# The mLSTM's queries and keys by seven-product groups, with the convolution in place

## The chip, the core and the metric

The kernel runs on one core of a Trainium2 chip. The metric is device time in microseconds (us) from launch to end. Five engines work side by side, each with its own queue of instructions that it takes strictly in the order written: TensorE (PE, matmul; its weight loads are shown as PEld), VectorE (DVE), ScalarE (ACT), GpSimd (POOL) and SyncE (SP), which issues the weight loads from main memory.

## The reference

A decoder trunk of two layers over 512 positions of width 1024, in float32. Cut to what matters here:

```python
for l in range(DEPTH):                                    # 2
    proj = x @ w_in[l]                                    # (512, 1024) @ (1024, 8200)
    (r_q, r_k, r_v, r_g, m_qk, m_v, m_o, m_i, m_f, g_a, g_b) = split(proj)
    # retention: 4 heads, rotary on r_q and r_k, head norm, silu(r_g), projection -> y_ret
    qk_c = silu(causal_depthwise_conv(m_qk, conv_w[l], conv_b[l]))   # width 4, along positions
    mq, mk = qk_c[..., :512], qk_c[..., 512:]             # 4 heads of 128
    # mLSTM: 4 heads of 128 x 256, head norm, sigmoid(m_o), projection -> y_ml
    mix = (sigmoid(g_a + b) * y_ret + sigmoid(g_b + b) * y_ml) @ w_out[l]
    x = layer_norm(alpha * x + mix)
    hidden = silu(gate) * up                              # x @ w_gate_up, 2 x 2816 columns
    x = layer_norm(alpha * x + hidden @ w_down[l])
```

## The kernel before

**Precision.** A number is split into two parts, hi (a cast on ScalarE, L201 for weights) and lo (number minus hi, a subtraction on the vector engine in `lo_of`, L133). A product is three matmuls: hi·hi, hi·lo, lo·hi. The weights come as 512 KB units (tile wraw) and are split into whi and wlo, four units ahead of their use (`LOOK = 4`).

**Three forms of product.** `feat` (L260 to L262) takes one unit and makes 128 output features for all 512 positions, laid out with features on partitions: 24 matmuls of 512 columns. `tok_units` (L351 to L353) makes 512 features with positions on partitions, four units for four PSUM banks. `quad` (L318) takes four units at once as a 2 x 2 block matrix and forms the product of 512 input halves and position halves with seven block products instead of eight (the scheme of Strassen and Winograd): 7 x 24 matmuls of 256 columns. Its operands are two weight blocks as they are, B11 and B22, further B21, and the sums T1, T3, T2 (vector engine, L187, L189, L191) and T4 (GpSimd, L223). Its other side needs four sums of the input (tiles xs, made by `input_sums`), and its results are put together from the banks as they come (for the merge gate in `gate_ev`, tiles ga and gc). Before, `quad` serves the merge gates and the feed-forward projection.

**The stages of a layer.** For two pairs of heads each: retention's q and k (4 `feat`, rotated by `rot_evac`: tiles rqk, rt), its values (`tok_units`, split into rvh and rvl), its gate (`tok_units`). Then the same for the mLSTM: q and k (4 `feat`, each with its convolution in `conv_evac`: one copy, four vector steps, one Silu), values (mvh, mvl), gate. Then the merge gates (4 `quad`), the two output projections, W_out, layer norm, feed-forward, layer norm. A stage of `tok_units` uses the four PSUM banks of the stage ahead of it, so its first matmul waits until that stage's first block is evacuated.

**Side work.** What belongs to a head (scores, weighted sums, head norm, the loads of head outputs in `fetch`, the input sums) is written as generators in the queue `side`. The stages call `slot()` after each piece of matmul work (six matmuls in `tok_units`, six to twelve in the others), and each call advances the first generator by one step. In one layer, `input_sums` stands in this queue behind the first head's scores of retention's second pair. It has four quarters, each with two additions on GpSimd (L577, tile xs), four small vector operations (L583, tile sf), a cast on ScalarE (tile xs0h or xs1h) and a split (xs0l, xs1l).

**What sets the order.** On TensorE and SyncE the instructions stand as the program writes them. On the other three a scheduler puts them in order when the program is built, except inside the `quad` stages, where these too stand as written.

The lines shown have the numbers of the kernel before; those of the kernel after differ by a few (L133 is the same; L577 is L586, L583 is L592, L610 is L618, L741 and L745 are L747 and L751, L853 is L886).

Of the kernel before, what the change touches and what calls it, by code (L numbers as in the profile page):

```python
# [15 lines left out]
P = 128  # L16
# [37 lines left out]
def layer_plan():  # L54
# [34 lines left out]
    for j in range(2, FT, 2):  # L89
        for c in (0, DFF):  # L90
# [7 lines left out]
NUNIT = len(layer_plan())  # L98
QUADS = [layer_plan().index(("F", w, c + j * P)) for w, c, js in (("in", O_GA, (0, 4)), ("in", O_GB, (0, 4)),
                                                                  ("gu", 0, range(2, FT, 2))) for j in js]  # L100
UNIT_IF = layer_plan().index(("F", "if", 0))
# [3 lines left out]
def decoder_trunk(ctx: ExitStack, tc: tile.TileContext, wall, xT_in, x_in, pvec, lnp, rtab, out):  # L105
# [18 lines left out]
    def scratch(shape, name):  # L124
        return reg.tile(shape, F32, tag="sc", name=name, bufs=4)
# [115 lines left out]

    side = deque()

    def slot():
        while side:
            try:
                next(side[0])
                return
            except StopIteration:
                side.popleft()  # L250
# [120 lines left out]
    def tok_blocks(pms, sh, sl, kts, first, evac, within):  # L371

        ws = [take() for _ in kts]
        for b in range(NB):
# [8 lines left out]
            evac(b, pms[b])  # L383

    K8 = [(2 * i, 2 * i + 1) for i in range(KT // 2)]

# [159 lines left out]
    def fetch(od, his, los):  # L546

        for i in range(4):
            t = scratch([P, 2, S], "of")
            nc.gpsimd.dma_start(t, od[:, 2 * i : 2 * i + 2])  # L550
            yield
            yield
            hi, lo = (x[i // 2][:, 2 * i % 4 : 2 * i % 4 + 2] for x in (his, los))
            nc.scalar.copy(hi, t)
            yield
            lo_of(lo, t, hi)
            yield
# [13 lines left out]
    def input_sums(xh, xl, sh, sl):  # L571

        t1, t2 = slice(0, S // 2), slice(S // 2, S)
        for m in range(4):
# [6 lines left out]
            for i, a, b, op in ((0, a21, a22, ALU.subtract), (1, f[:, 0], a11, ALU.subtract),  # L581
                                (2, a11, a21, ALU.subtract), (3, f[:, 1], a12, ALU.add)):
                nc.vector.tensor_tensor(out=f[:, i], in0=a, in1=b, op=op)  # L583
            yield
            nc.scalar.copy(sh[:, :, m], f)
# [3 lines left out]
    def rest(n):  # L589
        for _ in range(n):  # L590
            yield

    for l in range(L):
# [70 lines left out]

        for p in range(2):
            qk = reg.tile([P, 4, S], F32, tag="qk", name="rqk")
            rots = [rot_evac(qk[:, i]) for i in range(4)]
# [27 lines left out]
            side.append(scores(qk, 0, boxes[0], *ret_weights(2 * p)))  # L695
            if p == 1:
                side.append(input_sums(xh, xl, *xs))
            if p == 0:
# [35 lines left out]

        def conv_evac(dst, ct):
            def ev(pm):
                cw = lambda i: pv[:, C_CW + 4 * ct + i : C_CW + 4 * ct + i + 1]
                u = scratch([P, 2, S], "cv")
                r, t = u[:, 0], u[:, 1]
                nc.scalar.copy(r, pm)  # L740
                nc.vector.tensor_scalar(out=t, in0=r, scalar1=cw(3), scalar2=pv[:, C_CB + ct : C_CB + ct + 1],  # L741
                                        op0=ALU.mult, op1=ALU.add)
                for i in (2, 1, 0):
                    d = 3 - i
                    nc.vector.scalar_tensor_tensor(out=t[:, d:], in0=r[:, : S - d], scalar=cw(i), in1=t[:, d:],  # L745
                                                   op0=ALU.mult, op1=ALU.add)
                nc.scalar.activation(dst, t, AF.Silu)  # L747
            return ev

        for p in range(2):  # L750
            qk = reg.tile([P, 4, S], F32, tag="qk", name="mqk")  # L751
            for i in range(4):
                feat(xh, xl, conv_evac(qk[:, i], (i % 2) * 4 + 2 * p + i // 2))
            boxes = [[None], [None]]
# [106 lines left out]

        ordered = {mybir.EngineType.Activation, mybir.EngineType.DVE, mybir.EngineType.Pool}
        with tc.manual_schedule(engines=ordered):
            for m in (0, 4):
                quad(xh, xl, *xs, gate_ev(sga, 0, m))
# [332 lines left out]
```

## Time and profile before

| | us |
|---|---|
| three runs | 1804.14, 1806.07, 1806.31 (median 1806.07) |
| profiled execution | 1806.1 (span of its instructions 1804.4) |
| TensorE busy | 1772.4 (98% of the span) |
| VectorE busy | 1263.8 (70%) |
| ScalarE busy | 794.3 (44%) |
| GpSimd busy | 420.6 (23%) |

An engine's busy share is a mean over stages of different kinds. What counts is where TensorE stands still and which engine it waits for there. In the rows, "out<-in" names the tiles, "x" counts instructions, and square brackets give the idle time ahead of an instruction with the engine (and tile) that ended it. Matmuls overlap, so the distance of two starts, not the duration of one, is the time that a matmul takes.

### The profile page before, as it was taken

The numbers are of one execution on the slowest core, as the hardware profiler recorded it, in microseconds if no ns is written. First come the engines' busy times: TensorE is split into PE (matmuls) and PEld (weight loads), VectorE is DVE, ScalarE is ACT, GpSimd is POOL, SyncE is SP. The second block draws the span as 40 slices with busy tenths as digits, with TensorE's granted clock in tenths as the row PEclk, the third lists the DMA queues.
The fourth block names the chain that finished last, engine by engine and source line by source line (L and its number), as shares of the span: only waits on it lengthen the run. The fifth ranks groups of instructions, "written<-read, shape, count | busy, mean of one in ns | idle before, by whom it ended". The sixth has DMA issues, their size and how long they took to land.

```text
span 1804.4 us, 26440 instructions
## 1 busy us (share of the span) xinstructions
PE 1772.4 (98%) x10616; PEld 1580.5 (88%) x10616; DVE 1263.8 (70%) x1686; ACT 794.3 (44%) x1148; POOL 420.6 (23%) x309
## 2 busy tenths in 40 slices
PE   9998999999999999999999999999999999999997
PEld 7887888998889999988898788889988899999886
DVE  6676666775459999963476856667755599999534
ACT  4434655554225444452244345556532254444410
POOL 2041100231001455620120400012310015554200
PEclk9999999999999999999999999999999999999999
DMA  7332322247332333362243233213463333333521
GB/s 247 91 97 94 109 79 94 71 140 248 98 116 89 127 95 101 106 214 94 86 160 94 93 99 112 89 64 117 127 236 101 109 106 94 106 118 106 198 70 47
DMA packets 72826, 209.43 MB, mean 116 GB/s; under 512 B 6616, under 2 KB 8536, under 8 KB 71680
## 3 DMA queue, kind: packets, MB, share of 16 engines
q1 hardware_dynamic: 62864, 168.32, 29.0%
q0 software_dynamic: 9840, 39.43, 6.4%
q8 instruction: 83, 1.36, 0.3%
q14 instruction: 39, 0.32, 0.1%
HBM read 190.93 MB, written 16.79 MB: 115 GB/s over the span
## 4 chain that ended last, share of the span: by engine, by line
PE 92%; DVE 5%; issue 1%; ACT 1%; DMA 1%; POOL 0%; SPq 0%; DVEq 0%; ACTq 0%
PE pm L318 25%; PE pm L351 9%; PE pm L352 8%; PE pm L353 8%; PE pm L262 7%; PE pm L260 7%; PE pm L261 7%; PE pa L318 4%; PE pa L352 3%; PE pa L351 3%; PE pa L353 3%; DVE wlo L133 1%; DVE sf L583 1%; PE pa L484 1%; PE pa L485 1%; PE pa L486 1%
## 5 line engine op out<-in xcount | busy, mean ns | idle before, releaser
L133 DVE TENSOR_TENSOR wlo<-wraw,whi 128x1024 fp32r<-128x1024 f32 (+2 forms) x404 | 569.8, 1423 | 231.3 <-ACT whi L201 228.8
L201 ACT CAST whi<-wraw 128x1024 fp32r<-128x1024 f32 x391 | 408.8, 1049 | 507.2 <-PE pm L261 133.9
L440 POOL TENSOR_TENSOR rs<-ve,nhalf 128x4 f32<-128x4 f32 (+1 forms) x32 | 32.2, 1006 | 525.1 <-DVE ve L439 525.1
L351 PE MATMUL pm<-whi,x0h 128*128 128x512 f32 x256 | 102.9, 402 | 8.2 <-DVE rvl L133 8.1
L351 PE MATMUL pm<-whi,x20h 128*128 128x512 f32 x256 | 103.2, 403 | 7.0 <-DVE rvl L133 7.0
L353 PE MATMUL pm<-wlo,x20h 128*128 128x512 f32 x256 | 100.9, 394 | 0.0
L352 PE MATMUL pm<-whi,x20l 128*128 128x512 f32 x256 | 100.8, 394 | 0.0
L353 PE MATMUL pm<-wlo,x0h 128*128 128x512 f32 x256 | 100.7, 393 | 0.0
L352 PE MATMUL pm<-whi,x0l 128*128 128x512 f32 x256 | 100.5, 393 | 0.0
L223 POOL TENSOR_TENSOR wraw<-wraw 128x1024 f32<-128x1024 f32 x28 | 67.4, 2408 | 110.1 <-issue 54.4
L1049 POOL TENSOR_TENSOR qa<-qa 128x512 f32<-128x512 f32 x20 | 42.8, 2141 | 142.5 <-DVE qa L1048 90.6
L318 PE MATMUL pm<-s1h,wlo 128*128 128x256 f32 x240 | 67.9, 283 | 0.0
L318 PE MATMUL pm<-x10h,whi 128*128 128x256 f32 x240 | 67.9, 283 | 0.0
L318 PE MATMUL pm<-x10h,wlo 128*128 128x256 f32 x240 | 67.9, 283 | 0.0
L318 PE MATMUL pm<-s0h,whi 128*128 128x256 f32 x240 | 67.9, 283 | 0.0
L318 PE MATMUL pm<-x11h,whi 128*128 128x256 f32 x240 | 67.9, 283 | 0.0
L318 PE MATMUL pm<-x10l,whi 128*128 128x256 f32 x240 | 67.9, 283 | 0.0
L318 PE MATMUL pm<-s0l,whi 128*128 128x256 f32 x240 | 67.9, 283 | 0.0
L318 PE MATMUL pm<-x11l,whi 128*128 128x256 f32 x240 | 67.9, 283 | 0.0
L318 PE MATMUL pm<-s1h,whi 128*128 128x256 f32 x240 | 67.9, 283 | 0.0
L318 PE MATMUL pm<-s0h,wlo 128*128 128x256 f32 x240 | 67.9, 283 | 0.0
L318 PE MATMUL pm<-x11h,wlo 128*128 128x256 f32 x240 | 67.9, 283 | 0.0
(511 smaller groups left out, 5573.3 us busy)
## 6 DMA issues: line engine op xcount, KB each, us to landing
wraw<-wall SPq DMA_DIRECT2D x307, 512.0 KB, 3.7
od<-ot POOLq DMA_DIRECT2D x16, 512.0 KB, 3.0
of<-od POOLq DMA_DIRECT2D x16, 512.0 KB, 4.9
gb<-lnp POOLq DMA_DIRECT2D x4, 1024.0 KB, 6.5
x1d<-xr POOLq DMA_DIRECT2D x8, 512.0 KB, 2.9
xr<-x1d POOLq DMA_DIRECT2D x8, 512.0 KB, 4.7
negm<-md POOLq DMA_DIRECT2D x2, 1026.0 KB, 7.1
xr<-xtok POOLq DMA_DIRECT2D x4, 512.0 KB, 6.6
```

Of the source, the lines that this page charges most:

```text
L133: nc.vector.tensor_tensor(out=out_lo, in0=full, in1=hi.bitcast(F32), op=ALU.subtract)
L201: nc.scalar.copy(hi, sum_t[i])
L223: nc.gpsimd.tensor_tensor(out=raw_t[u + 2], in0=raw_t[u], in1=raw_t[u + 3], op=ALU.add)
L260: nc.tensor.matmul(pm[:, c0:c1], lhsT=hi[:, k], rhs=xh[:, k, c0:c1], start=(k == 0), stop=False)
L261: nc.tensor.matmul(pm[:, c0:c1], lhsT=hi[:, k], rhs=xl[:, k, c0:c1], start=False, stop=False)
L262: nc.tensor.matmul(pm[:, c0:c1], lhsT=lo[:, k], rhs=xh[:, k, c0:c1], start=False, stop=(k == KT - 1))
L318: nc.tensor.matmul(pm, lhsT=x[:, j, k], rhs=y[:, k], start=go and n == 0, stop=j == 1 and k == 3 and n == 2, skip_group_check=not first)
L351: nc.tensor.matmul(pm, lhsT=sh(k)[:, a], rhs=hi[:, j], start=first, stop=False)
L352: nc.tensor.matmul(pm, lhsT=sl(k)[:, a], rhs=hi[:, j], start=False, stop=False)
L353: nc.tensor.matmul(pm, lhsT=sh(k)[:, a], rhs=lo[:, j], start=False, stop=last)
L440: nc.gpsimd.tensor_tensor(out=rs[:, :n], in0=ve[:, :n], in1=nhalf[:, :n], op=ALU.pow)
L1049: nc.gpsimd.tensor_tensor(out=v, in0=v, in1=u, op=ALU.subtract)
```

## The change

Four things:

1. The mLSTM's q and k of a pair of heads are made by one `quad` instead of four `feat`. `conv_ev` puts the results together in the tile mqk; then `conv` runs over each of the four blocks, reads mqk and writes its Silu back to the same place. The copy ahead of each convolution is gone. A `rest(7)`, seven empty steps, stands in the side queue ahead of the scores.
2. `input_sums` goes to a queue of its own, `slow`, which every fifth call of `slot()` advances. It is put there at the start of retention's second pair, four projections earlier than before. One of its three yields per quarter is gone.
3. `fetch` has one more empty step between load and cast, and one more behind the cast.
4. `QUADS` lists the mLSTM's blocks, so their units are loaded as four blocks of the 2 x 2 matrix; number and size of the loads stay.

```diff
-QUADS = [... (("in", O_GA, (0, 4)), ("in", O_GB, (0, 4)), ("gu", 0, range(2, FT, 2))) for j in js]
+QUADS = [... (("in", O_MQK, (0, 2)), ("in", O_GA, (0, 4)), ("in", O_GB, (0, 4)), ("gu", 0, range(2, FT, 2))) for j in js]
...
-    side = deque()
+    side, slow = deque(), deque()
+    SLOW = 5
+    turn = {"n": 0}
 
     def slot():
+        turn["n"] += 1
+        if slow and turn["n"] % SLOW == 0:
+            if next(slow[0], "end") == "end":
+                slow.popleft()
         while side:
...
             nc.gpsimd.dma_start(t, od[:, 2 * i : 2 * i + 2])
             yield
             yield
+            yield
             hi, lo = (x[i // 2][:, 2 * i % 4 : 2 * i % 4 + 2] for x in (his, los))
             nc.scalar.copy(hi, t)
+            yield
             yield
             lo_of(lo, t, hi)
...
                 nc.vector.tensor_tensor(out=f[:, i], in0=a, in1=b, op=op)
-            yield
             nc.scalar.copy(sh[:, :, m], f)
             lo_of(sl[:, :, m], f, sh[:, :, m])
...
         for p in range(2):
+            if p == 1:
+                slow.append(input_sums(xh, xl, *xs))
             qk = reg.tile([P, 4, S], F32, tag="qk", name="rqk")
...
             side.append(scores(qk, 0, boxes[0], *ret_weights(2 * p)))
-            if p == 1:
-                side.append(input_sums(xh, xl, *xs))
...
-        def conv_evac(dst, ct):
-            def ev(pm):
-                u = scratch([P, 2, S], "cv")
-                r, t = u[:, 0], u[:, 1]
-                nc.scalar.copy(r, pm)
...
+        def conv(x, ct):
+            cw = lambda i: pv[:, C_CW + 4 * ct + i : C_CW + 4 * ct + i + 1]
+            t = scratch([P, S], "cv")
+            nc.vector.tensor_scalar(out=t, in0=x, scalar1=cw(3), scalar2=pv[:, C_CB + ct : C_CB + ct + 1],
+                                    op0=ALU.mult, op1=ALU.add)
+            for i in (2, 1, 0):
+                d = 3 - i
+                nc.vector.scalar_tensor_tensor(out=t[:, d:], in0=x[:, : S - d], scalar=cw(i), in1=t[:, d:],
+                                               op0=ALU.mult, op1=ALU.add)
+            nc.scalar.activation(x, t, AF.Silu)
+
+        def conv_ev(qk):
+            t = {}
+            part = lambda i, h: qk[:, 2 * i : 2 * i + 2, h * HC : (h + 1) * HC]
+            two = lambda bank: bank.rearrange("p (j t) -> p j t", j=2)
+
+            def ev(name, banks):
+                if name == "p1":
+                    t["u"] = scratch([P, 2, 2, HC], "mu")
+                    nc.scalar.copy(t["u"][:, 0], two(banks["a"]))
+                elif name == "p5":
+                    nc.scalar.copy(t["u"][:, 1], two(banks["c"]))
+                elif name == "p7":
+                    nc.vector.tensor_tensor(out=part(1, 1), in0=t["u"][:, 1], in1=two(banks["d"]), op=ALU.subtract)
+                elif name == "p6":
+                    u, v = t["u"][:, 0], t["u"][:, 1]
+                    nc.vector.tensor_tensor(out=u, in0=two(banks["b"]), in1=u, op=ALU.add)
+                    nc.gpsimd.tensor_tensor(out=v, in0=v, in1=u, op=ALU.subtract)
+                    nc.gpsimd.tensor_tensor(out=part(1, 1), in0=part(1, 1), in1=u, op=ALU.subtract)
+                elif name == "p2":
+                    nc.scalar.copy(part(0, 0), two(banks["a"]))
+                    nc.vector.tensor_tensor(out=part(1, 0), in0=two(banks["e"]), in1=t["u"][:, 1], op=ALU.add)
+                elif name == "p4":
+                    nc.vector.tensor_tensor(out=part(0, 1), in0=two(banks["d"]), in1=t["u"][:, 0], op=ALU.add)
             return ev
 
         for p in range(2):
             qk = reg.tile([P, 4, S], F32, tag="qk", name="mqk")
+            with tc.manual_schedule(engines=ordered):
+                quad(xh, xl, *xs, conv_ev(qk))
             for i in range(4):
-                feat(xh, xl, conv_evac(qk[:, i], (i % 2) * 4 + 2 * p + i // 2))
+                conv(qk[:, i], (i % 2) * 4 + 2 * p + i // 2)
+            side.append(rest(7))
```

What this makes of the order at three places. First GpSimd, layer 0, from the rotations of retention's second pair (L610 before, L618 after) to the end of the input sums (xs). Before:

```order
L610 TENSOR_TENSOR rqk<-rqk,rt 128x512 x2
L543 DMA od<-ot 128x1024
L610 TENSOR_TENSOR rqk<-rqk,rt 128x512
L543 DMA od<-ot 128x1024
L610 TENSOR_TENSOR rqk<-rqk,rt 128x512
L577 TENSOR_TENSOR xs<-x0h,x0l 128x512 x8
```

After:

```order
L586 TENSOR_TENSOR xs<-x0h,x0l 128x512 x2
L447 TENSOR_TENSOR rs<-ve,nhalf 128x4
L618 TENSOR_TENSOR rqk<-rqk,rt 128x512
L586 TENSOR_TENSOR xs<-x0h,x0l 128x512
L618 TENSOR_TENSOR rqk<-rqk,rt 128x512
L586 TENSOR_TENSOR xs<-x0h,x0l 128x512
L550 DMA od<-ot 128x1024
L618 TENSOR_TENSOR rqk<-rqk,rt 128x512
L550 DMA od<-ot 128x1024
L618 TENSOR_TENSOR rqk<-rqk,rt 128x512
L586 TENSOR_TENSOR xs<-x0h,x0l 128x512 x4
```

Four of the eight additions have moved between the rotations; the other four still follow the last rotation in one piece.

Second the vector engine, layer 0, first pair of the mLSTM, from the last convolution steps (cv) to the first split of the values (mvl). Before, the end of the fourth convolution is mixed with the scores (pf, pp, qf):

```order
L741 TENSOR_SCALAR cv<-cv,pv_98 128x512
L762 TENSOR_SCALAR pf<-negm,cols 128x128
L745 SCALAR_TENSOR_TENSOR cv<-cv,pv_98 128x511
L133 TENSOR_TENSOR wlo<-wraw,whi 128x1024
L745 SCALAR_TENSOR_TENSOR cv<-cv,pv_98 128x510
L769 SCALAR_TENSOR_TENSOR pf<-pa,pf 128x384
L745 SCALAR_TENSOR_TENSOR cv<-cv,pv_98 128x509
```

After, from the group's last evacuation:

```order
L777 TENSOR_TENSOR mqk<-pm,mu 128x2x256
L747 TENSOR_SCALAR cv<-mqk,pv_98 128x512 x2
L751 SCALAR_TENSOR_TENSOR cv<-mqk,pv_98,cv 128x511 x2
L751 SCALAR_TENSOR_TENSOR cv<-mqk,pv_98,cv 128x510 x2
L751 SCALAR_TENSOR_TENSOR cv<-mqk,pv_98,cv 128x509 x2
L747 TENSOR_SCALAR cv<-mqk,pv_98 128x512 x2
L751 SCALAR_TENSOR_TENSOR cv<-mqk,pv_98,cv 128x511 x2
L751 SCALAR_TENSOR_TENSOR cv<-mqk,pv_98,cv 128x510 x2
L751 SCALAR_TENSOR_TENSOR cv<-mqk,pv_98,cv 128x509 x2
L133 TENSOR_TENSOR wlo<-wraw,whi 128x1024 x2
L795 TENSOR_SCALAR pf<-negm,cols 128x256
```

All sixteen steps now stand in one piece behind the last evacuation, two chains side by side, and the scores behind them.

Third the vector engine, layer 0, end of the third group of the merge gates, where the third or fourth head output load (of) is split (orl). Before:

```order
L853 TENSOR_TENSOR ga<-pm,ga 128x512
L133 TENSOR_TENSOR orl<-of,orh 128x1024
L133 TENSOR_TENSOR wlo<-wraw,whi 128x1024 x4
L843 TENSOR_TENSOR gc<-ga,pm 128x512
L133 TENSOR_TENSOR wlo<-wraw,whi 128x1024
```

After:

```order
L886 TENSOR_TENSOR ga<-pm,ga 128x512
L133 TENSOR_TENSOR wlo<-wraw,whi 128x1024
L133 TENSOR_TENSOR orl<-of,orh 128x1024
L133 TENSOR_TENSOR wlo<-wraw,whi 128x1024 x3
L876 TENSOR_TENSOR gc<-ga,pm 128x512
L133 TENSOR_TENSOR orl<-of,orh 128x1024
```

One weight split has moved ahead of the load's split, and the last load's split (orl) has moved into the next group.

More of the change, by code (lines that the diff above doesn't have):

```diff
@@ L98 @@
 NUNIT = len(layer_plan())
-QUADS = [layer_plan().index(("F", w, c + j * P)) for w, c, js in (("in", O_GA, (0, 4)), ("in", O_GB, (0, 4)),
-                                                                  ("gu", 0, range(2, FT, 2))) for j in js]
+QUADS = [layer_plan().index(("F", w, c + j * P)) for w, c, js in (("in", O_MQK, (0, 2)), ("in", O_GA, (0, 4)),
+                                                                  ("in", O_GB, (0, 4)), ("gu", 0, range(2, FT, 2))) for j in js]
 UNIT_IF = layer_plan().index(("F", "if", 0))
@@ L383, in tok_blocks @@
             evac(b, pms[b])
+    ordered = {mybir.EngineType.Activation, mybir.EngineType.DVE, mybir.EngineType.Pool}
     K8 = [(2 * i, 2 * i + 1) for i in range(KT // 2)]
@@ L732, in decoder_trunk @@
         nc.gpsimd.dma_start(negm, md.unsqueeze(0).broadcast_to([P, NH, S + 1]))
-        def conv_evac(dst, ct):
-            def ev(pm):
-                cw = lambda i: pv[:, C_CW + 4 * ct + i : C_CW + 4 * ct + i + 1]
-                u = scratch([P, 2, S], "cv")
-                r, t = u[:, 0], u[:, 1]
-                nc.scalar.copy(r, pm)
[L741 to L747, printed above, removed]
+        def conv(x, ct):
[8 more added lines that the diff above has]
+            nc.scalar.activation(x, t, AF.Silu)
@@ L860, in gate_ev @@
             return ev
-        ordered = {mybir.EngineType.Activation, mybir.EngineType.DVE, mybir.EngineType.Pool}
         with tc.manual_schedule(engines=ordered):
+            assert not slow
             for m in (0, 4):
```

## Prediction

> **What bounds the kernel now.** I read the page first, then the waits of the tensor engine, then busy time by stage, last the rows around the places where the tensor engine stands still. The page:
>
> ```profile
> PE 1772.4 (98%) x10616; PEld 1580.5 (88%) x10616; DVE 1263.8 (70%) x1686; ACT 794.3 (44%) x1148; POOL 420.6 (23%) x309
> PE 92%; DVE 5%; issue 1%; ACT 1%; DMA 1%; POOL 0%; SPq 0%; DVEq 0%; ACTq 0%
> ```
>
> The tensor engine sets the end; the vector engine holds 5% of the chain that ended last. So a change pays by taking matmul time away, or a stop of the tensor engine. What it waits for (us in total, times, longest):
>
> ```profile
> PE pm L351 <- DVE rvl L133: 15.1, 4, 6.4
> PE pa L318 <- DVE wlo L133: 2.8, 2, 1.7
> ```
>
> The first row is mostly the start of retention's gate stage for the second pair of heads: its PSUM banks come free only when the vector engine has split the values (rvl). By stage (busy PE, PEld, DVE, ACT, POOL, then granted clock and DMA), first that pair's projections, then what follows, for layer 0 and layer 1:
>
> ```profile
> 93.80:117.50 23.70, 23.70 (x114) 19.60 (x113) 12.38 (x18) 9.57 (x14) 9.10 (x6) 1.00 0.35 110
> ...
> 117.50:140.60 23.10, 23.10 (x106) 19.21 (x105) 22.61 (x29) 7.20 (x10) 14.46 (x9) 1.00 0.22 71
> 140.60:147.20 6.60, 0.40 (x2) 0.00 (x0) 6.60 (x10) 4.76 (x7) 0.00 (x0) 0.73 0.35 93
> 147.20:152.00 4.80, 4.61 (x17) 3.87 (x18) 3.48 (x6) 1.54 (x3) 0.00 (x0) 0.67 0.45 158
> ...
> 1032.70:1039.30 6.60, 0.43 (x2) 0.00 (x1) 6.60 (x10) 4.74 (x7) 0.00 (x0) 0.89 0.40 94
> 1039.30:1050.00 10.70, 10.49 (x45) 9.02 (x46) 4.73 (x10) 2.96 (x6) 0.00 (x0) 0.75 0.25 89
> ```
>
> The vector engine has room during the projections (12.38 of 23.70), is full with the input sums (22.61 of 23.10, then all of 6.60), and the tensor engine stops:
>
> ```profile
> 140.62 0.39 PE L353 MATMUL pm<-wlo,x0h 128*128 128x512 f32 x1
> 147.39 0.79 PE L351 MATMUL pm<-whi,x0h 128*128 128x512 f32 x1 [6.38 <-DVE rvl L133]
> ```
>
> From 140.62 to 147.39, less the 0.23 us that one matmul takes here, are 6.5 us; layer 1's window looks the same. Then the granted clock is 0.67 over 4.80 us and 0.75 over 10.70 us, another 1.6 and 2.7 us. Lost: 8.1 + 9.2 = 17.3 us.
>
> Why the vector engine is that late: the sums' first step runs on GpSimd beside it.
>
> ```profile
> 122.27 3.03 POOL L577 TENSOR_TENSOR xs<-x0h,x0l 128x512 f32<-128x512 f32 x2
> ...
> 124.07 1.51 DVE L583 TENSOR_TENSOR sf<-xs 128x256 f32<-128x256 f32 x1
> 129.16 0.42 DVE L583 TENSOR_TENSOR sf<-sf,xs 128x256 f32<-128x256 f32 x1
> ```
>
> The same kind of subtraction takes 0.42 us alone and 1.51 beside an addition: each addition on GpSimd costs the vector engine about 1.1 us.
>
> **The change, part by part.** *The seven-product groups.* 96 matmuls of 512 columns become 168 of 256. Both forms stand in the trace with the same 16 transposes of a head norm between them: the mLSTM's q|k stage (first row) and the first group of the merge gate (third row):
>
> ```profile
> 179.75:203.41 23.66, 23.66 (x114) 19.59 (x112) 15.45 (x24) 12.89 (x23) 2.17 (x3) 1.00 0.37 120
> 203.41:226.00 22.59, 22.59 (x104) 18.79 (x103) 13.45 (x24) 15.51 (x28) 3.08 (x8) 1.00 0.32 100
> ...
> 335.60:357.50 21.90, 21.90 (x186) 21.90 (x185) 18.79 (x25) 14.95 (x24) 5.95 (x4) 1.00 0.28 90
> ```
>
> 23.66 − 21.90 = 1.76 us, for four groups (two pairs, two layers): **−7.0 us**. The Trainium skill ("TensorE: Matmul & The Clock Gate", section "Wait — 56ns, not 53.3ns?") gives a matmul its columns at 2.4 GHz and about 2.5 ns more; by that the estimate would be 4 × (96 × 215.8 − 168 × 109.2 ns), 9.5 us. The rows here show less, and the rows count.
>
> A group needs three more operands, each with a cast on ScalarE and a split on the vector engine, four weight sums (one on GpSimd), four evacuations and two GpSimd subtractions. The gate's first group does exactly this beside a head norm: 18.79 of 21.90 us of the vector engine, and the tensor engine is busy for all of it. That cover costs nothing; were it gone, each late split would cost what it costs in layer 0's gates below, 1.2 us. The first sums fall into the stages ahead, which have room or hold them already (second row: before the gates):
>
> ```profile
> 152.00:179.75 27.75, 27.75 (x151) 23.96 (x150) 14.14 (x35) 13.27 (x26) 1.87 (x4) 1.00 0.30 103
> ...
> 303.90:335.60 31.70, 31.70 (x172) 27.28 (x171) 22.92 (x65) 13.63 (x24) 3.44 (x2) 1.00 0.07 24
> ```
>
> *The input sums.* By the order shown ahead, four of their eight GpSimd additions (xs) now stand between the rotations, and four still come in one piece. The vector engine so loses from the full stretch a quarter of the sums (four subtractions and a split, 4 × 0.42 + 1.2 = 2.9 us) and the collisions of four additions (4 × 1.1 = 4.4). 7.3 us is more than the 6.5 us by which it was late; what moves finds 11.3 us of room in the projections. Since the last two quarters still stand ahead of rvl, I leave a stop of 1.0 us per layer, short enough for the clock to stay up: 17.3 − 2.0, **−15.3 us**. Bounds: −17.3; and −5.8 if only the 2.9 us per layer go and the collisions move along.
>
> *The convolution.* Each of the 16 chains is as before (0.54 + 2.32 us):
>
> ```profile
> 187.40 0.54 DVE L741 TENSOR_SCALAR cv<-cv,pv 128x512 f32<-128x512 f32 x1
> 187.97 2.32 DVE L745 SCALAR_TENSOR_TENSOR cv<-cv,pv 128x511 f32<-128x511 f32 x3
> ...
> 204.93 1.28 ACT L765 ACT_TABLE_LOAD   x1
> ...
> 212.91 0.41 DVE L133 TENSOR_TENSOR pp<-qf,pp 128x256 fp32r<-128x256 f32 x1
> ```
>
> But where three of four lay under the matmuls of the q|k stage, now all four (4 × 2.9 = 11.6 us) begin after the last product. Let T be the group's end on the tensor engine. The first head's q and k are ready at about T + 0.7 + 5.8 + 0.6 + 1.0 + 0.6 = T + 8.7 (evacuation, two chains side by side, a Silu, a weight cast, the other Silu). The tensor engine asks for them after 54 matmuls, T + 12.3: rest(7) covers it by 3.6 us. The next thing that can be late is the split of the values, which frees the first bank for the gate stage at T + 22.6 (203.41 to 226.00). Until then the vector engine has 13.45 us of work today; minus the fourth chain (2.9), plus four chains and an evacuation (12.3), that is 22.85 us for 22.6: full. And it can't run without waits: the score chain, table load to last split, takes 204.93 to 213.32, 8.4 us. It starts at T + 0.7 + 11.6 + 0.6 + 1.0 = T + 13.9 and ends at T + 22.3; with the next head's four Exp (1.1), a value cast (0.6), a weight split (1.2) and the value split (0.7), all in turn, T + 25.9, or 3.3 us late. Bounds per stage: 0 (the chains overlap fully) and 3.3. Queued behind are only this stage's values and scores; weights are split four units ahead. Near the full sum I take 1.2 us, four times: **+4.8 us**.
>
> *The head output loads.*
>
> ```profile
> 402.46 0.56 POOL L550 DMA_DIRECT2D of<-od  x1
> ...
> 407.28 1.05 ACT L554 CAST orh<-of 128x1024 fp32r<-128x1024 f32 x1
> ...
> 408.36 1.23 DVE L133 TENSOR_TENSOR orl<-of,orh 128x1024 fp32r<-128x1024 f32 x1 [3.02 <-ACT orh L554]
> 409.50 4.62 DVE L133 TENSOR_TENSOR wlo<-wraw,whi 128x1024 fp32r<-128x1024 f32 x4
> ```
>
> The vector engine waits 3.02 us for a load, with four weight splits queued behind; the first is late and the tensor engine stops (the 2.8 us of the second wait, once per layer). Now one weight split stands ahead of that load's: it can run at about 405.4, four us before the tensor engine asks for it. **−2.8 us**; bounds 0 and −2.8. The loads now take 24 of 28 slots, and the last piece is asked for only some 4 us into the next stage, so their own lateness stays covered.
>
> **The sum.** The profiled execution took 1806.1 us (span 1804.4), the median shown 1806.07, so no correction. 1806.1 − 7.0 − 15.3 + 4.8 − 2.8 = 1785.8: **1786 us**.
>
> **The rivals.**
> 1. *The values are split late.* The chain behind the convolution runs in turn: 3.3 instead of 1.2 us per stage, +8.4: 1794. For it: 22.85 us in 22.6. Against it: two of ScalarE's table loads go, since all Silu now stand ahead of the Exp. Chance 0.18.
> 2. *The sums stay in the way.* −5.8 instead of −15.3: 1795. For it: half the additions in one piece, just ahead of rvl. Against it: 7.3 us moved, 6.5 late. Chance 0.12.
> 3. *GpSimd holds up the vector engine.* Each group brings three more GpSimd additions; at 1.1 us each, all on the path, 12 × 1.1 = +13.2: 1799. Against it: the gate's groups have them too, and the tensor engine doesn't stop. The Trainium skill ("SBUF — State Buffer", section "Who interferes with whom") speaks for this one: a vector instruction with two SBUF inputs and a GpSimd instruction that reads SBUF exclude each other, and the convolution's three steps are of that kind; the pair of 0.42 and 1.51 us agrees. Chance 0.06.
> 4. *Slower.* Place: the vector engine's queue at the end of each group, in written order. If its evacuations lie L us behind the products there, convolution and value split shift whole: four times L. Layer 0's gates show such lateness (the four splits at 409.50). With L = 7, 28 us: 1814; it decides from L = 6 on, where it eats the gain. Against it: 18.79 of 21.90 in the same group with a head norm. Chance 0.04.
> 5. *Nothing net*: the sums' stop reappears in the first group, whose operands it feeds, 20 us again: 1806. The sums end well ahead of it by the slots (40 of 48). Chance 0.03.
>
> The forecast has 0.57. Its own range: 1779 (no new stop, all 17.3 us from the sums) to 1791 (the value stop twice as long). Below I add 1 us for rounding in the terms; rivals 1 to 3 widen it upward: **1778 to 1799**. A measurement of this kernel can tell about 0.2%, 3.6 us, from no change. Faster: 0.57 + 0.18 + 0.12 + 0.06 = 0.93; same 0.03; slower 0.04.
>
> **What will show it.** The q|k stages of the mLSTM at 21.9 us with no idle inside; the wait on rvl at some 1 to 3 us instead of 15.1, and the granted clock at 1.00 after it; a new wait on mvl of about 1 us, four times; no wait on wlo in the gates. Wrong I am if the wait on mvl exceeds 3 us, if the additions still stretch the subtractions ahead of rvl to 1.5 us throughout, or if the tensor engine waits for mqk after the 54 matmuls.

## The result and the profile after

| | before | after |
|---|---|---|
| median of the timed runs | 1805.43 us (4 runs, 1804.14 to 1806.31) | 1778.21 us (4 runs, 1776.74 to 1779.65) |
| span of the profiled execution | 1804.4 us | 1776.2 us |

The ratio is 0.985, with a 95% interval of 0.9833 to 0.9867: 27.2 us or 1.5% faster. Forecast were 1786 us and a range of 1778 to 1799; the time lies at the range's lower edge, and the change brought 7 to 8 us more than the 20.3 that I gave it (27.2 by the medians, 28.2 by the spans).

The engines' busy times and the chain that ended last, on the page of the kernel after:

```profile
PE 1759.9 (99%) x10904; PEld 1586.3 (89%) x10904; DVE 1312.9 (74%) x1726; ACT 793.6 (45%) x1148; POOL 433.3 (24%) x321
...
PE 97%; DVE 1%; ACT 0%; issue 0%; DMA 0%; SPq 0%; DVEq 0%
```

The vector engine has 49 us more to do than before (1312.9 against 1263.8), and yet its share of the chain fell from 5% to 1%. What the tensor engine still waits for, the two largest of five rows that come to 6.3 us in all (us in total, times, longest):

```profile
PE pm L357 <- DVE rvl L133: 2.3, 2, 1.7
PE pm L344 <- ACT whi L430: 1.9, 1, 1.9
```

The 15.1 us on rvl are 2.3 (one short stop per layer behind the mLSTM gates' logits, at the gate stage of retention's first pair; the kernel before has them as well), the 2.8 us on wlo in the merge gates are gone, and the wait on mvl that I forecast is not there.

Now by stage. The windows begin and end at the first matmul of a stage (us, busy PE, PEld, DVE, ACT, POOL, then granted clock, DMA share, GB/s). Before: values and gate of retention's second pair in layer 0 and layer 1, an mLSTM q|k stage and the values and gate behind it, the merge gates of both layers:

```profile
117.50:179.75 62.25, 55.87 (x273) 47.04 (x272) 46.84 (x78) 26.77 (x45) 16.33 (x13) 0.95 0.29 94
1009.62:1072.88 63.26, 56.88 (x273) 47.91 (x272) 46.83 (x78) 27.19 (x47) 16.33 (x13) 0.95 0.29 92
...
203.41:257.68 54.27, 54.27 (x274) 46.05 (x273) 33.61 (x91) 30.94 (x56) 4.34 (x11) 1.00 0.27 84
335.60:419.27 83.67, 82.62 (x689) 82.41 (x688) 64.06 (x66) 51.47 (x78) 29.42 (x20) 1.00 0.46 150
1228.72:1313.47 84.75, 82.84 (x689) 82.46 (x688) 64.72 (x66) 51.98 (x79) 29.43 (x20) 1.00 0.46 147
```

The same stages after:

```profile
116.97:171.24 54.27, 54.27 (x273) 46.08 (x272) 42.01 (x73) 24.91 (x43) 11.42 (x10) 1.00 0.24 81
996.33:1050.58 54.25, 54.25 (x273) 46.08 (x272) 42.00 (x73) 25.44 (x43) 12.01 (x10) 1.00 0.27 85
...
171.24:193.05 21.81, 21.81 (x186) 21.81 (x184) 15.01 (x20) 14.32 (x22) 4.14 (x4) 1.00 0.54 159
193.05:247.43 54.38, 54.38 (x276) 46.14 (x274) 44.69 (x105) 28.56 (x53) 7.07 (x13) 1.00 0.21 73
...
323.61:405.98 82.37, 82.37 (x689) 82.36 (x688) 69.34 (x67) 52.15 (x78) 28.38 (x20) 1.00 0.47 155
1202.95:1285.32 82.37, 82.37 (x690) 82.36 (x688) 69.61 (x68) 52.20 (x78) 29.81 (x20) 1.00 0.46 156
```

In every row after, PE is busy for the whole window at a clock of 1.00. The account:

| part | forecast | measured | from |
|---|---|---|---|
| groups, with the stages behind them (all four alike) | −7.0 | −6.9 | 4 × (21.81 − 23.65 + 54.38 − 54.27) |
| input sums | −15.3 | −17.0 | 54.27 − 62.25 + 54.25 − 63.26 |
| values split late | +4.8 | 0 | no wait on mvl |
| head output loads | −2.8 | −3.7 | 82.37 − 83.67 + 82.37 − 84.75 |
| start of the kernel | 0 | −0.5 | first tokens at 36.02 instead of 36.52 |
| sum | −20.3 | −28.1 | the spans differ by 28.2 |

(The 23.65 of a q|k stage is the 23.66 of the prediction's row, from first matmul to first matmul.) The row on the start is chance: in the profiled executions of the kernels below the first token stage begins between 34.2 and 37.6 us, and the spread of the runs is of that size.

### The profile page after: what moved, and what is told of

Read it like the earlier page. It is cut to its first block, busy times and chain, and to the rows that moved or that the text cites. A ratio compares the mean times of both kernels' runs of the same rounds, so it can differ in the third digit from the quotient of the medians.

```text
span 1776.2 us, 27128 instructions
## 1 busy us (share of the span) xinstructions
PE 1759.9 (99%) x10904; PEld 1586.3 (89%) x10904; DVE 1312.9 (74%) x1726; ACT 793.6 (45%) x1148; POOL 433.3 (24%) x321
## 4 chain that ended last, share of the span: by engine, by line
PE 97%; DVE 1%; ACT 0%; issue 0%; DMA 0%; SPq 0%; DVEq 0%
PE pm L324 31%; PE pm L357 9%; PE pm L359 9%; PE pm L358 9%; PE pm L266 6%; PE pm L268 6%; PE pm L267 6%; PE pa L324 5%; PE pa L358 3%; PE pa L357 3%; PE pa L359 3%; PE pa L491 1%; PE pa L492 1%; PE pa L493 1%; PE pa L547 1%; PE pa L465 1%
## 5 line engine op out<-in xcount | busy, mean ns | idle before, releaser
L133 DVE TENSOR_TENSOR wlo<-wraw,whi 128x1024 fp32r<-128x1024 f32 (+2 forms) x416 | 599.6, 1453 | 203.1 <-ACT whi L201 200.5
L201 ACT CAST whi<-wraw 128x1024 fp32r<-128x1024 f32 x403 | 421.1, 1049 | 476.2 <-PE pm L267 116.0
L223 POOL TENSOR_TENSOR wraw<-wraw 128x1024 f32<-128x1024 f32 x32 | 77.0, 2405 | 150.9 <-issue 58.1
L324 PE MATMUL pm<-s1l,whi 128*128 128x256 f32 x240 | 67.9, 283 | 0.0
```

The lines of the kernel that those rows point to most:

```text
L133: nc.vector.tensor_tensor(out=out_lo, in0=full, in1=hi.bitcast(F32), op=ALU.subtract)
L201: nc.scalar.copy(hi, sum_t[i])
L223: nc.gpsimd.tensor_tensor(out=raw_t[u + 2], in0=raw_t[u], in1=raw_t[u + 3], op=ALU.add)
L324: nc.tensor.matmul(pm, lhsT=x[:, j, k], rhs=y[:, k], start=go and n == 0, stop=j == 1 and k == 3 and n == 2, skip_group_check=not first)
```

## The experiments

Two questions: does each part bring what the account gives it, and why was the vector engine in time where I had it late? The times of before beside each run lie between 1804.1 and 1806.1, so a difference to the kernel after, which ran beside another of them, is good to about 2 us.

**1. Only the sums back where they were.**

```diff
         for p in range(2):
-            if p == 1:
-                slow.append(input_sums(xh, xl, *xs))
...
             side.append(scores(qk, 0, boxes[0], *ret_weights(2 * p)))
+            if p == 1:
+                side.append(input_sums(xh, xl, *xs))
```

> The changed kernel with the input sums back in the queue of side work, behind the first head's scores; groups and load spreading stay. My theory (the early start takes the sums and their collisions out of the vector engine's full stretch): the stop ahead of retention's gate stage comes back with 6.5 us per layer, the granted clock falls after it, 17 us in all: 1795 us. Rival (the groups themselves emptied the vector engine, the place of the sums matters little): under 1783 us, stop under 2 us per layer.

Measured: 1793.57 us (ratio 0.9936, 0.992 to 0.9951), 15.4 more than the kernel after. The wait is back as it was:

```profile
PE pm L357 <- DVE rvl L133: 15.1, 4, 6.4
```

What follows: the sums' place is worth some 15 to 17 us (by the stages 62.59 and 62.49 instead of 54.27 and 54.25), and the groups and the loads together some 11. The rival (under 1783 us) falls.

**2. Only the groups undone** (four `feat` with `conv_evac` for each pair of heads, no `rest(7)`, `QUADS` as before; that is the kernel before with parts 2 and 3 of the change). The heart of the edit:

```diff
-            with tc.manual_schedule(engines=ordered):
-                quad(xh, xl, *xs, conv_ev(qk))
             for i in range(4):
-                conv(qk[:, i], (i % 2) * 4 + 2 * p + i // 2)
-            side.append(rest(7))
+                feat(xh, xl, conv_evac(qk[:, i], (i % 2) * 4 + 2 * p + i // 2))
```

> The changed kernel with the mLSTM's queries and keys by four single products and the convolution per product again; the sums stay spread. My theory (the groups are worth 1.73 us each and bring no new stop): 1778.2 + 6.9 = 1785 us, every other stage as in the changed kernel. Rival (the sums' gain depends on the groups): the stop on rvl comes back, 1795 us or more.

Measured: 1784.57 us (ratio 0.9884, 0.9867 to 0.9901), 6.4 more than after, and no new wait. What follows: the groups are worth their matmul time, 7 us, and nothing of it is given back.

**3. Only the fetch steps undone.**

```diff
             yield
             yield
-            yield
             hi, lo = (x[i // 2][:, 2 * i % 4 : 2 * i % 4 + 2] for x in (his, los))
             nc.scalar.copy(hi, t)
-            yield
             yield
```

> The changed kernel with the head output loads stepped as before (two empty steps ahead of the cast, one behind it). My theory: the merge gates' four groups take 83.7 and 84.7 us again instead of 82.4, +3.7 us: 1782 us, with a wait on wlo in the gates of about 1.2 and 1.9 us. Rival (the wait went since work ahead of the gates moved): 82.4 us stays, 1778 us.

Measured: 1780.15 us (ratio 0.9865, 0.9848 to 0.9881), 1.9 more than after, which the runs alone don't tell from nothing. The trace does: the gates take 84.03 and 83.51 us instead of 82.37, together 2.8 (I expected 3.7), and the wait of before is back, with the vector engine held by a load and four weight splits queued behind it, as before:

```profile
PE pa L324 <- DVE wlo L133: 2.3, 2, 1.4
```

```profile
399.86 1.23 DVE L133 TENSOR_TENSOR orl<-of,orh 128x1024 fp32r<-128x1024 f32 x1 [3.27 <-ACT orh L561]
```

**4. The kernel before, with the sums' eight additions on the vector engine.** Why was rvl late: because the vector engine had too much to do of its own there, or because GpSimd held it up?

```diff
-                nc.gpsimd.tensor_tensor(out=t[:, i], in0=xh[:, m + 4 * i].bitcast(F32), ..., op=ALU.add)
+                nc.vector.tensor_tensor(out=t[:, i], in0=xh[:, m + 4 * i].bitcast(F32), ..., op=ALU.add)
```

> The kernel before, with the input sums' eight additions on the vector engine instead of GpSimd, nothing else. My theory (each GpSimd addition costs the vector engine 1.1 us, more than the 0.6 us that the addition takes on the vector engine itself): the stop on rvl shrinks from 6.5 us by about 4 per layer, and the clock stays up after it: 1794 to 1797 us. Rival (the vector engine is late by the amount of its own work): eight additions more make it 4.8 us later per layer, 1815 us.

Measured: 1788.45 us (ratio 0.9906, 0.9889 to 0.9924). With eight more instructions on the engine that was late, the stop is gone altogether (both stages 54.25 us). Its rows:

```profile
122.46 0.68 DVE L577 TENSOR_TENSOR xs<-x0h,x0l 128x512 f32<-128x512 f32 x1
...
136.78 1.28 DVE L133 TENSOR_TENSOR rvl<-pm,rvh 128x512 fp32r<-128x512 f32 x2
137.97 0.75 DVE L583 TENSOR_TENSOR sf<-xs 128x256 f32<-128x256 f32 x2
```

An addition takes the vector engine 0.68 us; on GpSimd it cost the vector engine 1.1 us of waiting. The own-work rival (1815 us) falls. The stop that I still expected is absent since the order, made anew at the build, puts two value splits ahead of the last quarter's subtractions. Counted from the stage's start, the first value split ends at 22.3 us instead of 29.8. Of these 7.5 us, 3.6 are work that now stands behind it (a weight split, the last quarter's four subtractions and its split, by the distance of their starts). The other 3.9 are what the additions' move brings, close to the 8 × (1.1 − 0.6) that I expected; neither part alone covers the 6.5 us of the stop.

**5. The kernel after, sums at the old place and their additions on the vector engine** (the edits of 1 and 4 together): is the queue of its own needed at all?

```diff
-                nc.gpsimd.tensor_tensor(out=t[:, i], in0=xh[:, m + 4 * i].bitcast(F32), ..., op=ALU.add)
+                nc.vector.tensor_tensor(out=t[:, i], in0=xh[:, m + 4 * i].bitcast(F32), ..., op=ALU.add)
...
-                slow.append(input_sums(xh, xl, *xs))
...
+                side.append(input_sums(xh, xl, *xs))
```

> The changed kernel with the input sums back at their old place in the side queue (as in the experiment that gave 1793.6 us and two stops of 6.6) and their eight additions on the vector engine instead of GpSimd. Theory (the stop was the collisions of the two engines, 8 x 1.1 us; an addition costs the vector engine 0.65 us of its own): no stop on rvl in either layer, the two stages 54.25 us, the groups 21.8 us, about 1778 us, as with the queue of its own. Rival (beside the groups the sums are needed earlier than in the kernel before, where the first group came 100 us later; the sums of the last quarter, which stand behind the first value splits in that order, are late for the mLSTM's first group): a stop on xs0l or xs1l at the start of the first group, 1780 to 1786 us.

Measured: 1777.41 us (1777.32 to 1778.8; ratio 0.9845, 0.9828 to 0.9861), the same as the kernel after within what can be told. The two stages take 54.75 and 54.71 us, half a microsecond more than after:

```profile
PE pm L357 <- DVE rvl L133: 2.7, 4, 1.7
```

What follows: one word in one line (the engine of the additions) does what the slow queue does. Here all subtractions of the sums still stand ahead of the first value split, and only a weight split and the sums' last split (2.3 us) have gone behind it. It ends 23.7 us behind the stage's start instead of 29.8, so 3.9 us are again the additions' own. The rival (late sums for the first group) falls; the first group takes 21.80 us.

**6. Spread, but begun late.** The slow queue is filled behind the scores, and advanced at every third slot.

```diff
-    SLOW = 5
+    SLOW = 3
...
-            if p == 1:
-                slow.append(input_sums(xh, xl, *xs))
...
             side.append(scores(qk, 0, boxes[0], *ret_weights(2 * p)))
+            if p == 1:
+                slow.append(input_sums(xh, xl, *xs))
```

> The changed kernel with the spread sums put in their queue only behind the projections of retention's second pair, on every third slot. My theory (the early start and the collisions count, not the spreading as such): by the built order all eight GpSimd additions and three quarters of the sums still lie ahead of rvl, so only 2.9 us of vector work leave: a stop of 3 to 4 us per layer, 1785 to 1791 us. Rival (spreading is enough): no stop, 1778 us.

Measured: 1790.36 us (ratio 0.9911, 0.9896 to 0.9926), with stops on rvl of 3.9 and 4.6 us. Spreading alone is not enough; that half of the additions left the stretch is what counts. The vector engine shows it in layer 0:

```profile
143.46 1.88 DVE L133 TENSOR_TENSOR rvl<-pm,rvh 128x512 fp32r<-128x512 f32 x3
```

Ahead of this first value split stands the same vector work as in the kernel after (three quarters of the sums, four weight splits, the scores), but beside eight additions instead of four. The split ends 27.2 us behind the stage's start instead of 23.1: four additions cost 4.1 us.

**7. Begun early, but not spread.** The slow queue advances at every slot.

```diff
-    SLOW = 5
+    SLOW = 1
```

> The changed kernel, but the sums in the slow queue take a step at every slot instead of every fifth, from the same early start: all four quarters lie in the projections of the second pair of heads. Theory (what counts is that the additions on GpSimd are out of the stretch in which the values are split; the even spacing is worth nothing by itself): no stop on rvl at 140, the second token stage 54.25 us in both layers, about 1778 us as the changed kernel, and the last rvl done earlier than 0.5 us before it is asked for. Rival (packed, the additions hold up the weight splits of the projections): a stop on wlo between 93 and 117, projections longer than 23.7 us, 1781 to 1786 us.

Measured: 1780.8 us (ratio 0.9862, 0.9845 to 0.9878). The first value split now ends 2.5 us ahead of the need and both stages take 54.25 us, as the theory had it, but neither expectation is right as a whole: the order reaches back into the stage ahead, and there a split beside an addition is late. GpSimd, vector engine and tensor engine, layer 0:

```profile
79.42 2.83 POOL L586 TENSOR_TENSOR xs<-x0h,x0l 128x512 f32<-128x512 f32 x2 [1.17 <-DVE pp L133]
```

```profile
81.03 2.31 DVE L133 TENSOR_TENSOR wlo<-wraw,whi 128x1024 fp32r<-128x1024 f32 x1
```

```profile
83.65 0.39 PE L493 MATMUL pa<-rvh,pp 128*128 128x256 f32 x1 [0.62 <-DVE pp L480]
```

The weight split takes 2.31 us instead of 1.2, and the weighted sums wait for pp. In layer 1 that stage takes 56.99 us against 55.51 after, in layer 0 58.70 against 57.28. So the even spacing is worth about 1.5 us per layer: it keeps the collisions apart from work that has no room for them.

**8. Without `rest(7)`.**

```diff
-            side.append(rest(7))
```

> The changed kernel without the seven empty steps ahead of the mLSTM's scores. My theory: the tensor engine asks for q and k after 12 matmuls, 2.7 us behind the group's end, and has them at 7.1 us: a stop of 4.4 us in each of four stages, 17.6 us, and some more if the clock falls after it: 1796 to 1802 us. Rival (the scheduler puts the first chains earlier, or the scores' place has slack): under 1783 us.

Measured: 1799.84 us (6 runs; ratio 0.9965, 0.9951 to 0.9978), 21.6 more than after. The wait, and the window behind the first stop:

```profile
PE pa L465 <- ACT mqk L753: 15.4, 4, 4.5
```

```profile
198.30:203.00 4.70, 4.70 (x17) 3.85 (x17) 4.70 (x11) 0.63 (x1) 0.00 (x0) 0.64 0.00 0
```

The first head's q and k (two of the four chains, with their Silu) are what the tensor engine would wait for; the seven empty steps let value matmuls go first. Of 23.0 us lost in the four stages, 16.1 are the stops themselves (3.42, 4.62, 3.42 and 4.61 from start to start), the rest is mostly the clock, 0.64 over the 4.70 us that follow.

**9. One vector step more in each of the 16 chains** (it takes the larger of the tile and itself).

```diff
+            nc.vector.scalar_tensor_tensor(out=t, in0=t, scalar=1.0, in1=t, op0=ALU.mult, op1=ALU.max)
             nc.scalar.activation(x, t, AF.Silu)
```

> The changed kernel with one more vector step in each convolution chain, which leaves its value as it is: four steps of 0.67 us, 2.7 us per stage. Theory after the result (the first value split ends 1.4 us ahead of the need): the margin is used up and 1.3 us per stage show, four times: 1783 us. Rival (the forecast on record, the vector engine is full and every us shows): 4 x 2.7 = 10.8 us, 1789 us. Third: the margin is larger than the rows show, since the order is made anew: 1778 us.

Measured: 1778.27 us (ratio 0.9843, 0.9829 to 0.9858), no new wait: 2.6 us more per stage cost nothing. The first two expectations fall, for both hold the order fixed; the third (the order is made anew) held. The first value split ends 0.7 us ahead of the need instead of 2.2: the second head's qf and part of its pf, which stand ahead of the first value split or between the splits in the kernel after, now stand behind three of them.

**10. Three steps more.**

```diff
+            for _ in range(3):
+                nc.vector.scalar_tensor_tensor(out=t, in0=t, scalar=1.0, in1=t, op0=ALU.mult, op1=ALU.max)
             nc.scalar.activation(x, t, AF.Silu)
```

> The changed kernel with three vector steps more in each of the 16 convolution chains (each takes the maximum of the tile and itself, so the values stay), about 12 x 0.65 = 7.8 us more on the vector engine between the group's end and the value splits, four times. One step more (2.6 us) was absorbed: the order was made anew and the first value split ended 22.7 us after the group, just at the need. Theory (the value split is the next thing to be late, and the order has little left to move behind it): the q|k operands are not late, since their two chains side by side end about 4 us later against a cover of 3.6, at most a short stop there; mvl comes 3 to 6 us late at the gate stage in each of four stages, the clock falls after it by another 1 to 2, together 16 to 30 us: 1794 to 1808 us. Rival (the order moves more of the second head's work behind the splits, and the tensor engine waits for nothing): 1778 to 1783 us, no stop on mvl over 1 us.

Measured: 1782.56 us (ratio 0.9874, 0.9859 to 0.9889), 4.4 more than after. Now the stop is there, and it is small. The waits, then the vector engine and the tensor engine in the first such stage:

```profile
PE pa L492 <- DVE mvl L133: 3.9, 4, 1.0
```

```profile
200.24 3.70 DVE L754 SCALAR_TENSOR_TENSOR cv<-cv 128x512 f32<-128x512 f32 x6
...
216.92 0.69 DVE L133 TENSOR_TENSOR mvl<-pm,mvh 128x512 fp32r<-128x512 f32 x1
217.52 1.02 DVE L804 SCALAR_TENSOR_TENSOR pf<-pa,pf 128x384 f32<-128x384 f32 x2
...
220.51 1.88 DVE L133 TENSOR_TENSOR mvl<-pm,mvh 128x512 fp32r<-128x512 f32 x3
```

```profile
218.25 0.39 PE L357 MATMUL pm<-whi,x0h 128*128 128x512 f32 x1
...
221.24 0.39 PE L492 MATMUL pa<-mvl,pp 128*128 128x258 f32 x1 [0.98 <-DVE mvl L133]
```

Twelve steps (7.4 us, twice 3.70) were added, 1.2 us are lost per stage. The first split, which frees the bank, ends at 217.61 for the 218.25 at which the gate stage starts; what is late is the second one, for the weighted sums. The scores now stand on both sides of the first split. The theory named the right tile, at the wrong place and at four to seven times its price. The rival had time and price right (up to 1783 us, no stop over 1 us), but not that the tensor engine waits for nothing.

**11. The four chains one after another**, in the order of the program.

```diff
-            for i in range(4):
-                conv(qk[:, i], (i % 2) * 4 + 2 * p + i // 2)
+            with tc.manual_schedule(engines={mybir.EngineType.DVE}):
+                for i in range(4):
+                    conv(qk[:, i], (i % 2) * 4 + 2 * p + i // 2)
```

> The changed kernel with the four convolution chains written one behind the other on the vector engine instead of two side by side. My theory (a step behind its own predecessor starts about 0.1 us later than one behind another chain's, which is why four chains took 10.1 us and not the 11.6 of the forecast): steps 0.77 us apart again, the chains' end 1.5 us later, just the margin of 1.4 us, so 1778 to 1780 us. Rival (the steps are shorter since their input is no longer a copy in scratch): 0.67 us apart here too.

Measured: 1779.46 us (1776.72 to 1781.03; ratio 0.985, 0.9835 to 0.9865), no wait on mvl. Three steps that follow each other take, by the vector engine's timeline,

```profile
201.10 2.32 DVE L751 SCALAR_TENSOR_TENSOR cv<-mqk,pv,cv 128x511 f32<-128x511 f32 x3
```

0.77 us each, as before the change. So the shorter time of the chains in the kernel after comes from their standing side by side. It was not what saved the stage: with the chains in turn the first value split still ends 1.4 to 1.5 us ahead of the need.

## Why the prediction was right, and where it was wrong

The time came out inside the range by luck as much as by reckoning. With every part at its favourable bound the sum gives 1779 us, and that is about where the parts came out; only the 1 us added for rounding puts 1778.2 inside. Two terms were wrong, both on the same side.

**The bound and the groups: right.** The four q|k stages take 21.81 us; 21.90 were read from the gates' first group. −6.9 against −7.0, and undone alone (experiment 2) 6.4. The cover named for the vector engine's extra work held: 15.01 of 21.81 us.

**The sums: the mechanism right, the remaining stop wrong.** GpSimd, layer 0, after:

```profile
75.49 2.86 POOL L586 TENSOR_TENSOR xs<-x0h,x0l 128x512 f32<-128x512 f32 x2
...
104.87 1.30 POOL L586 TENSOR_TENSOR xs<-x0h,x0l 128x512 f32<-128x512 f32 x1 [2.23 <-DVE sf L592]
...
124.75 2.93 POOL L586 TENSOR_TENSOR xs<-x0h,x0l 128x512 f32<-128x512 f32 x2 [3.88 <-DVE xs0l L133]
129.37 2.72 POOL L586 TENSOR_TENSOR xs<-x0h,x0l 128x512 f32<-128x512 f32 x2 [1.69 <-DVE pp L133]
```

Four additions have left the full stretch, but not all to the place that I gave them: two stand between the rotations (at 104.87 and 111.05), and two are done in the gate stage ahead, at 75.49 us. The four that come late still stretch what runs beside them (the split at 126.45 to 2.31 us, the one of pp at 129.41 to 1.53). The vector engine's first value split, in the kernel before and in the kernel after, and the matmul after that needs the bank:

```profile
146.65 1.88 DVE L133 TENSOR_TENSOR rvl<-pm,rvh 128x512 fp32r<-128x512 f32 x3
```

```profile
139.39 1.88 DVE L133 TENSOR_TENSOR rvl<-pm,rvh 128x512 fp32r<-128x512 f32 x3
```

```profile
140.32 0.39 PE L357 MATMUL pm<-whi,x0h 128*128 128x512 f32 x1
```

Three splits in 1.88 us, each of 0.69 in a row; the first ends at 140.08, 0.24 us ahead of the need (0.35 in layer 1). Counted from the stage's start it ends at 23.1 us instead of 29.8, 6.7 us earlier. The arithmetic had 7.3: 2.9 for the quarter of the sums, of which 2.6 came in layer 0, and 4.4 for the four additions, of which 4.1 came (experiment 6 has the one without the other). So it was right to within 0.6, and against 6.5 us late it said that the split would be in time. It was close all the same: experiments 1 and 6 show what the stop costs once it is there. "I leave a stop of 1.0 us per layer" had no row behind it; this is the step that failed. What was to be had was 17.0 us by the stages (17.3 by the clock's windows), and all of it came, 1.7 more than the sum gave. The sign "some 1 to 3 us" for the wait on rvl was met by luck: the 2.3 are the two stops behind the logits.

**The values split late: the term that failed.** "+4.8 us" stood for a chain that would end at T + 25.9 if all ran in turn, for a need at T + 22.6. Measured, with T = 193.05:

```profile
193.62 1.00 DVE L747 TENSOR_SCALAR cv<-mqk,pv 128x512 f32<-128x512 f32 x2
194.54 4.05 DVE L751 SCALAR_TENSOR_TENSOR cv<-mqk,pv,cv 128x511 f32<-128x511 f32 x6
...
199.42 4.04 DVE L751 SCALAR_TENSOR_TENSOR cv<-mqk,pv,cv 128x511 f32<-128x511 f32 x6
...
210.98 0.42 DVE L133 TENSOR_TENSOR pp<-qf,pp 128x256 fp32r<-128x256 f32 x1
...
213.62 0.69 DVE L133 TENSOR_TENSOR mvl<-pm,mvh 128x512 fp32r<-128x512 f32 x1
```

```profile
206.06 1.28 ACT L798 ACT_TABLE_LOAD   x1 [0.99 <-issue]
```

```profile
205.40 0.59 PE L465 MATMUL pa<-mqk 128*128 128x256 f32 x2
...
216.51 0.39 PE L357 MATMUL pm<-whi,x0h 128*128 128x512 f32 x1
```

Step by step, in us behind T:

| | predicted | measured |
|---|---|---|
| chains and last Silu, to the table load | 13.9 | 13.0 (206.06) |
| score chain, table load to last split | 8.4 | 5.3 (to 211.40) |
| next head's Exp, value cast, weight split, value split | 3.6 | 2.9 (to 214.31) |
| first value split done | 25.9 | 21.3 |
| the gate stage asks for the bank | 22.6 | 23.5 (216.51) |

The largest error is the score chain. Its 8.4 us were read from the kernel before, where it ran mixed with the fourth convolution. These are rows from inside that chain, vector engine and then ScalarE:

```profile
205.61 0.75 DVE L745 SCALAR_TENSOR_TENSOR cv<-cv,pv 128x511 f32<-128x511 f32 x1
...
207.41 0.77 DVE L745 SCALAR_TENSOR_TENSOR cv<-cv,pv 128x510 f32<-128x510 f32 x1
...
208.84 0.74 DVE L745 SCALAR_TENSOR_TENSOR cv<-cv,pv 128x509 f32<-128x509 f32 x1
```

```profile
209.75 1.28 ACT L747 ACT_TABLE_LOAD   x1
```

With the first step (0.55 at 204.95) they are 2.8 us of convolution on the vector engine, which I had counted already in the 11.6 us ahead; and the table load for its Silu stands in ScalarE's queue ahead of the last casts. The chain without them is the 5.3 us measured. The chains took 9.8 us (193.62 to 203.38, where the next instruction starts) instead of 11.6. And the need was misread: in the kernel before, the gate stage's first matmul stands at 226.75, T + 23.3 with that kernel's T of 203.41, and not at 226.00, the end of the window that I took; the change moved it by 0.1. Together the split is 2.2 us early instead of 3.3 late. One row of the kernel before would have warned me, its first value split, here with the matmul that needs the bank:

```profile
223.52 0.68 DVE L133 TENSOR_TENSOR mvl<-pm,mvh 128x512 fp32r<-128x512 f32 x1
```

```profile
226.75 0.39 PE L351 MATMUL pm<-whi,x0h 128*128 128x512 f32 x1
```

It ended at T + 20.8. My sum made the change move it by 5.1 us; it moved by 0.5. My own first rival had the clue in it ("two of ScalarE's table loads go") and I used it against the rival only, not in the sum.

There is a second reason why such a sum was the wrong tool. It holds the order fixed, but outside the groups the order is made at the build from the program's dependences, and experiments 9 and 10 show it giving way: of 2.6 us added nothing was lost, of 7.4 only 1.2. So even a right sum would have been an upper bound.

**The first head's q and k: right, by more.** Forecast were T + 8.7 for a need at T + 12.3; both of the first head's Silu are done at T + 7.1 (200.15), the matmul comes at T + 12.35 (205.40). Without `rest(7)` this is the stop, as experiment 8 shows.

**The head output loads: right, a little small.** −3.7 against −2.8: from start to start the two stops on wlo are 1.2 and 1.9 us, and layer 1 had a third one of 0.4 us, on gc, that went with them; the stages lost 1.3 and 2.4. Undone alone it costs 2.8.

**The rivals.** "The values are split late" (1794) and "the sums stay in the way" (1795) did not happen; experiments 10 and 6 show kernels in which each begins. "GpSimd holds up the vector engine" fails for the groups: with 4.14 us of GpSimd in a stage of 21.81, the vector engine has 6.8 us to spare there; one weight split beside them takes 2.37 us, and the tensor engine doesn't wait for it. The rule of the Trainium skill that I named beside it ("SBUF — State Buffer", section "Who interferes with whom") is borne out by experiments 4 and 5 all the same: where the vector engine has no room, taking the eight additions off GpSimd brings the first value split 3.9 us earlier, although the vector engine then makes them itself. "Slower", with evacuations that lie L behind the group's end, has an L of 0.5: the last one runs from 192.89 to 193.58, T is 193.05. And of "nothing net" there is no trace: the first group has no stop, its 21.81 us are all busy.

## What to carry to other kernels

When a duration for a chain is read from a trace, look at what runs between its links there; what the change moves elsewhere must be taken out of the chain before both are added. Then compare the sum with where the same instruction ends in the kernel before. Where GpSimd and the vector engine share a full stretch, price an addition by what it costs the vector engine in waiting; if that is more than the addition takes on the vector engine itself, moving the engine is cheaper than moving the work. And where a scheduler orders the instructions, a sum over a fixed order is only a bound on lateness, as experiments 9 and 10 show for one place: I would now give such a term its low end unless the work that cannot move already exceeds the room.

## What was not expected of the hardware

- **Steps of the vector engine that wait on the step just ahead are slower by 0.1 us.** Three dependent steps take 2.32 us (0.77 each, experiment 11); the same steps of two chains side by side take 4.05 us for six (0.675 each). The Trainium skill ("VectorE: DVE Perf Modes", section "The DRAIN you can't avoid") says that the pipeline empties after every instruction and that a semaphore after each costs nothing extra, as measured there on eight copies. For these steps the rows show a difference, and the measurement decides.
- **The same short stop lowers the clock in some executions and not in others.** All kernels here have a stop of 1.9 us at about 60 us (the wait on rvl with 1.7 in the list). In 10 of the 13 profiled executions the clock stays up behind it, in three (experiments 3, 10 and 11) it falls, and the stage takes 58.7 us instead of 57.3 (that of experiment 7 is as long for the reason told there). The window behind the stop, in the kernel after and in that of experiment 10:

```profile
62.30:67.00 4.70, 4.70 (x25) 4.05 (x26) 3.39 (x6) 0.72 (x3) 0.00 (x0) 1.00 0.63 161
```

```profile
62.60:67.00 4.40, 4.40 (x16) 3.69 (x17) 3.25 (x6) 0.59 (x2) 0.00 (x0) 0.65 0.57 158
```

  Of the stops of 3.4 us and more, each one in the experiments lowered it: 0.64 after 3.42 us (experiment 8), and a stage with a stop of 3.93 us became 6.7 us longer (experiment 6). The Trainium skill ("TensorE: Matmul & The Clock Gate", section "What's actually happening") has a window of about 3.4 us that runs freely, and lets the clock fall after at least one idle window. The stops of 3.4 us and more agree; a stop of 1.9 us fills no such window and lowered the clock three times all the same, so there the measurement decides. That it depends on where in the window the stop falls is a guess that no run here tests. For a forecast in this kernel: that stop costs 2 us or, now and then, 3.4.
